# Moving the recurrence's decays, a weight's low parts and a pair's queries in the mixer of a decoder layer

## The chip, the cores and the metric

The kernel runs on one core of a Trainium2 chip. The metric is device time in microseconds (us) of one execution, the median over runs. Engines are named as in the profile: PE (TensorE, matrix products and transposes), PEld (its weight loads), DVE (VectorE), ACT (ScalarE), POOL (GpSimd), SP (SyncE, which issues DMA transfers).

## The reference

One layer of a decoder, on 512 tokens of 1024 channels, in float32: a SwiGLU feed-forward half step, a mixer, and a second half step, each between RMS norms. The change lies in the mixer, which joins a gated linear recurrence (RG-LRU, 512 channels) and sliding-window attention (8 query heads, 2 key and value heads of 64 channels, window 128, one sink per head):

```python
r = jax.nn.sigmoid(block_diag(xc, w_rg, b_rg))
i = jax.nn.sigmoid(block_diag(xc, w_ig, b_ig))
log_a = LRU_C * r * jax.nn.log_sigmoid(lam)
a = jnp.exp(log_a)
mult = jnp.sqrt(-jnp.expm1(2.0 * log_a))
u = mult * (i * xc)                     # h[t] = a[t] * h[t-1] + u[t]
...
scores = where(mask, q @ k_band * scale, MASK_VALUE)
m = jnp.maximum(jnp.max(scores), sink)
p = jnp.exp(scores - m)
out = (p / (jnp.sum(p) + jnp.exp(sink - m))) @ v_band
...
y_lru = h * jax.nn.gelu(gate_lru)
y = concatenate([rms_norm(y_lru, g_lru_out), rms_norm(out, g_attn_out)]) @ w_o
```

## The kernel before

Everything is kept transposed, channels on the 128 partitions and the 512 tokens along the free axis, so that one tile is 128x512. float32 products are made of three matmuls on rounded parts: a high part (a cast on ACT) and a low part (the value less its high part, on DVE) of the weight and of the input, as high by high, high by low, low by high (L407, L408, L409 in `mm3`).

**Weights.** They arrive by DMA into raw buffers, five of them, in a fixed order. `W.cast(n)` makes high parts on ACT (whi, L172) and `W.fill(n)` low parts on DVE (wlo, L177), up to n units beyond those taken by products. When the last unit of a raw buffer has been filled, the next load is issued on SP's queue.

**Order.** The schedule is manual: each engine runs its instructions in the order in which the program writes them, and semaphores alone hold one engine for another. So a statement's place in the program is its place in the queue of every engine that it uses.

**The recurrence** has four chunks of channels. `decay_a` (L1294) makes a = exp(ka r) on ACT and its square m on POOL (L1296); `decay_b` (L1299) makes (m + 1) th on DVE, `root` (L1302) its square root on ACT, `root_u` (L1305) multiplies it into the input on DVE, `scan` (L1308) runs the recurrence on DVE.

**Attention** runs in four pairs of heads, j = 0 to 3, with n = 0 and 1 for the two heads of a pair. `q_parts(j)` casts the queries out of PSUM (qTjh on ACT, L1313) and subtracts (qTjl on DVE, L1314). `products(j)` makes scores on PE (L1338). `scores` (L1344 to L1350) masks and takes maxima on DVE, `exps` (L1357, L1359) exponentiates on ACT, `normalise` (L1364 to L1366) scales on DVE. `turn_p` transposes on PE (L1374), copies to pa on ACT (L1376) and selects pc from it on POOL (L1377). `values(j)` multiplies by v (L1389 to L1396), `rows_high` and `rows_low` split the result into yah (ACT) and yal (DVE, L481), with squares (L438) summed in acc_attn (L1410).

**Fillers.** Between these steps PE runs the input products of later pairs and of gelu's gates, in the order pq2, gt0, pq3, gt1, gt2, gt3: `pump(n)` runs n steps of three matmuls each; eight steps make a product, and the eighth also issues `q_parts` (for a pq) or `gelu_a` (a copy and a square on ACT, L1419 and L1421, for a gt). `gelu_b` (L1424) and `gelu_d` are on DVE, `gelu_c` (tanh, L1427) on ACT.

**Tables.** ACT loads a table of functions when the next function isn't in the one loaded; `preload(f)` (L385) does so ahead of need, with an activation of one column. Exponential and tanh share a table, the square root has another.

After the last pair follow `values(3)`, the last gates, the norm of the recurrence's output, and the product with w_o (L1611), whose weights are also cast and split by W.

Of the kernel before, what the change touches and what calls it, by code (L numbers as in the profile page):

```python
# [11 lines left out]
AF = mybir.ActivationFunctionType  # L12
# [11 lines left out]
KC = C // P  # L24
# [97 lines left out]
def tile_layer(ctx: ExitStack, tc: tile.TileContext, out: bass.AP, **ins: bass.AP):  # L122
# [17 lines left out]
    def bank(name):  # L140
        return psum.tile([P, T], F32, tag="bank", name=name)

    def t2k(name, dt=F32):
        return big.tile([P, T], dt, tag="t2k", name=name, bufs=NT2K)

    def wt(name, w=T, dt=F32):
        return tmp.tile([P, w], dt, tag="w", name=name, bufs=NW)


    W = Weights()  # L150
# [233 lines left out]
    def preload(func):  # L384
        act.activation(dummy, eps, func)  # L385
# [25 lines left out]
    def product(w, xs, sl=ALL, name="", hooks=()):  # L411
        ps = bank(name)
        hooks = dict(hooks)
        for k, x in enumerate(xs):
            if k in hooks:
                hooks[k]()
            mm3(ps[:, sl], w, k, [t[:, sl] for t in x], k == 0, k == len(xs) - 1)
        return ps
# [829 lines left out]
    def in_product(name, hooks=(), ahead=AHEAD):  # L1248
        return product(W.take(ahead), mx.xs, name=name, hooks=hooks)
# [42 lines left out]
    def decay_a(ci):  # L1292
        a = rs_[ci]
        act.activation(a, a, AF.Exp, scale=ka[:, ci:ci + 1])  # L1294
        m = ms[ci] = wt(f"m{ci}")
        pool.tensor_mul(m, a, a)  # L1296

    def decay_b(ci):
        dve.scalar_tensor_tensor(th[ci], ms.pop(ci), 1.0, th[ci], op0=ALU.add, op1=ALU.mult)  # L1299

    def root(ci):
        act.activation(th[ci], th[ci], AF.Sqrt)  # L1302
# [16 lines left out]
    def q_parts(j, b):  # L1319
        qT[j] = in_parts(b, f"qT{j}")  # L1320
# [6 lines left out]
    def products(j):  # L1327

        for n in range(2):
            score_banks[j, n] = [bank(f"sc{j}{n}{i}") for i in range(2)]  # L1330
        (qh, ql), (kh, kl) = qT[j], kT
        rows = [slice(n * HD, (n + 1) * HD) for n in range(2)]
        for b in range(NB):
            i, o = ((1, 0), (0, 0), (0, 2 * P), (1, P))[b]
            blk, keys = slice(b * P, (b + 1) * P), slice(max(b - 1, 0) * P, (b + 1) * P)
            for p, (q_, k_) in enumerate(((qh, kh), (qh, kl), (ql, kh))):
                for n, pr in enumerate(rows):
                    pe.matmul(score_banks[j, n][i][:, o:o + keys.stop - keys.start], q_[pr, blk], k_[pr, keys], start=p == 0, stop=p == 2)  # L1338

    def scores(j, n):  # L1340
        h = n * KC + j
        mx_ = small.tile([P, NB], F32, tag="mx", name=f"mx{j}{n}")
        mid, ends = (t.rearrange("p (b k) -> p b k", k=P) for t in score_banks[j, n])
        dve.copy_predicated(mid[:, 1::2, :], up8[:, :2, :], mid[:, 0::2, :])  # L1344
        dve.tensor_reduce(mx_[:, 1:3], mid[:, 1::2, :], op=ALU.max, axis=AX.X)
        dve.copy_predicated(ends[:, 0, :], up8[:, 0, :], neg[:, :P])
        dve.copy_predicated(ends[:, 2, :], up8[:, 0, :], ends[:, 1, :])
        dve.tensor_reduce(mx_[:, 0::3], ends[:, 0::2, :], op=ALU.max, axis=AX.X)
        nm = small.tile([P, NB], F32, tag="nm", name=f"nm{j}{n}")
        dve.tensor_scalar(nm, mx_, -scale, nsink[:, h:h + 1], op0=ALU.mult, op1=ALU.min)  # L1350
        unit[j, n] = (ends[:, 0, :], mid[:, 1, :], mid[:, 3, :], ends[:, 2, :]), nm

    def exps(j, n):
        h, (blocks, nm) = n * KC + j, unit[j, n]
        den, es = (small.tile([P, NB], F32, tag=t, name=f"{t}{j}{n}") for t in ("den", "es"))
        sc = wt(f"sc{j}{n}")
        act.activation(es, nm, AF.Exp, bias=sinks[:, h:h + 1])  # L1357
        for b in range(NB):
            act.activation(sc[:, b * P:(b + 1) * P], blocks[b], AF.Exp, bias=nm[:, b:b + 1], scale=scale, accum_out=den[:, b:b + 1])  # L1359
        unit[j, n] = sc, den, es  # L1360

    def normalise(j, n):
        sc, den, es = unit[j, n]
        dve.tensor_add(den, den, es)  # L1364
        dve.reciprocal(den, den)
        dve.tensor_mul(v4(sc), v4(sc), den.unsqueeze(2).to_broadcast([P, NB, P]))  # L1366
        unit[j, n] = sc

    def turn_p(j, n):
        p = unit[j, n]  # L1370
        pt = bank(f"pt{j}{n}")
        for b in range(NB):
            bs = slice(b * P, (b + 1) * P)
            pe.transpose(pt[:, bs], p[:, bs], ident)  # L1374
        pa, pc = (t2k(f"{t}{j}{n}") for t in ("pa", "pc"))
        act.copy(pa, pt)  # L1376
        pool.affine_select(v4(pc)[:, 1:, :], v4(pa)[:, 1:, :], pattern=[[0, NB - 1], [1, P]], base=0, channel_multiplier=-1, compare_op=ALU.is_ge, fill=0.0)  # L1377
        unit[j, n] = pa, pc

    def values(j):  # L1380

        o = bank(f"po{j}")
        for b in range(NB):
            for n in range(2):
                pa, pc = unit[j, n]
                chans = slice(b * P + n * HD, b * P + (n + 1) * HD)
                keys, own = slice(b * P, min(b + 1 + (not b), NB) * P), slice(b * P, (b + 1) * P)
                if b:
                    pe.matmul(o[n * HD:(n + 1) * HD, own], vd[:, chans], pc[:, own], start=False, stop=b == NB - 1, skip_group_check=True)  # L1389
                else:  # L1390
                    pe.matmul(o[n * HD:(n + 1) * HD, keys], v[:, chans], pa[:, keys], start=True, stop=False, skip_group_check=True)
            for n in range(2):
                pa, pc = unit[j, n]
                chans, nxt = slice(b * P + n * HD, b * P + (n + 1) * HD), slice((b + 1) * P, (b + 2) * P)
                if 0 < b < NB - 1:
                    pe.matmul(o[n * HD:(n + 1) * HD, nxt], v[:, chans], pa[:, nxt], start=False, stop=False, skip_group_check=True)  # L1396
        po[j] = o

    def rows_high(j):
        ysp[KC + j] = t2k(f"yah{j}", F32R), t2k(f"yal{j}", F32R)  # L1400
        x_high(ysp[KC + j], po[j], col("g_attn_out", j), ALL)
        if j == 0:
            act.activation(acca, po[j], AF.Square)
        else:
            po["sq", j] = square(po[j], ALL, f"a{j}")

    def rows_low(j):
        x_low(ysp[KC + j], po[j], col("g_attn_out", j), ALL)
        if j:
            dve.tensor_add(acca, acca, po.pop(("sq", j)))  # L1410
# [44 lines left out]
    def pump(n):  # L1455
        for _ in range(n):
            next(steps, None)
# [24 lines left out]
    pv = in_product("pv", (), 0)  # L1482
    W.cast(2)
    preload(AF.Exp)
    for n in range(2):
        exps(0, n)
    vT = taken(wt("vT"), pv)
# [4 lines left out]
            pe.transpose(vt[:, b * P:(b + 1) * P], vT[:, b * P:(b + 1) * P], ident)  # L1492

    pq = in_product("pq1", {2: turn_v}, 0)
    normalise(0, 0)
    v, vd = t2k("v"), t2k("vd")
    dve.tensor_copy(v, vt)
    normalise(0, 1)
    W.fill(1)
    for ci in range(KC):  # L1500
        decay_a(ci)
    q_parts(1, pq)
    dve.tensor_sub(vd[:, P:], v[:, P:], v[:, :T - P])
    turn_p(0, 0)
    pump(1)
    turn_p(0, 1)
    products(1)
    W.cast(1)
    preload(AF.Sqrt)
    for ci in range(KC):  # L1510
        decay_b(ci)
        root(ci)
    W.fill(1)
    preload(AF.Exp)
    pump(4)

    after = {0: [(root_u, 0), (root_u, 1), (scan, 0)],
# [2 lines left out]
    for j in range(KC - 1):  # L1520
        for n in range(2):
            scores(j + 1, n)
            exps(j + 1, n)
        values(j)
        rows_high(j)
        W.fill(1)
        for n in range(2):
            normalise(j + 1, n)
        pump(4)
        W.cast(2)  # L1530
        rows_low(j)
        for fn, i in after[j]:
            fn(i)
        pump((5, 5, 6)[j])
        turn_p(j + 1, 0)
        pump(1)
        turn_p(j + 1, 1)
        if j < KC - 2:
            products(j + 2)
        W.fill(2)  # L1540
        pump(4)
# [191 lines left out]
```

## Time and profile before

| | |
|---|---|
| median of 3 runs | 861.47 us (861.0 to 862.05) |
| profiled execution | 859.76 us, of which span 857.7 us |
| granted TensorE clock, mean | 0.997 |
| busy shares of the span | PE 98%, PEld 90%, DVE 77%, ACT 62%, POOL 18% |
| instructions | 14130 |

The profile is one execution, seen by the hardware profiler; its span runs from the first instruction to the last, and the execution's own time is 2.06 us longer. In a row of a time line stand start (us from the span's start), duration, engine, line, operation, output<-inputs, shape and count; a count above 1 means that equal instructions in a row were put together, and the duration is then of all of them from the first start to the last end. In square brackets stands how long the engine had been idle before, and on what. In a row of the waits stand who waited, for whom, the total, the count and the mean. The mixer part that the change touches lies between about 395 and 460 us of the span.

### The profile page before, as it was taken

The numbers are of one execution on the slowest core, as the hardware profiler recorded it, in microseconds if no ns is written. First come the engines' busy times: TensorE is split into PE (matmuls) and PEld (weight loads), VectorE is DVE, ScalarE is ACT, GpSimd is POOL, SyncE is SP. The second block draws the span as 40 slices with busy tenths as digits, with TensorE's granted clock in tenths as the row PEclk, the third lists the DMA queues.
The fourth block names the chain that finished last, engine by engine and source line by source line (L and its number), as shares of the span: only waits on it lengthen the run. The fifth ranks groups of instructions, "written<-read, shape, count | busy, mean of one in ns | idle before, by whom it ended". The sixth has DMA issues, their size and how long they took to land.

```text
span 857.7 us, 14130 instructions
## 1 busy us (share of the span) xinstructions
PE 844.0 (98%) x5534; PEld 768.7 (90%) x5534; DVE 658.1 (77%) x897; ACT 529.1 (62%) x901; POOL 155.4 (18%) x185
## 2 busy tenths in 40 slices
PE   9999999999999999999989999999999999999996
PEld 8888999989989998998778889888998998998995
DVE  4989898887988866767888675357488789888856
ACT  6647567566566555658766776245466657657542
POOL 2022005014025021015203030001101303204412
PEclk9999999999999999999999999999999999999998
DMA  8265339739559463113060508244433946938912
GB/s 247 100 196 196 119 105 234 189 99 237 150 109 265 156 194 126 50 50 99 2 146 27 193 28 294 75 141 155 147 99 103 231 134 150 219 99 200 267 75 98
DMA packets 92901, 124.41 MB, mean 145 GB/s; under 512 B 5864, under 2 KB 62500, under 8 KB 92836
## 3 DMA queue, kind: packets, MB, share of 16 engines
q1 hardware_dynamic: 76276, 86.68, 32.5%
q0 software_dynamic: 16416, 36.71, 19.2%
q8 instruction: 43, 0.70, 0.3%
q14 instruction: 22, 0.18, 0.1%
q10 hardware_dynamic: 144, 0.13, 0.0%
HBM read 93.10 MB, written 30.41 MB: 144 GB/s over the span
## 4 chain that ended last, share of the span: by engine, by line
PE 90%; DVE 4%; ACT 3%; DMA 1%; SPq 1%; issue 0%; DVEq 0%; ACTq 0%
PE aa L817 12%; PE ab L817 11%; PE da L817 6%; PE db L817 5%; PE wo L1611 4%; PE ba L817 3%; PE bb L817 3%; PE mn L699 1%; PE an L699 1%; PE yal L1145 1%; PE yal L1146 1%; PE yb L1146 1%; PE yb L1144 1%; PE yal L1144 1%; PE yb L1145 1%; DMA raw_second<-in_ffn_w_gu 1%
## 5 line engine op out<-in xcount | busy, mean ns | idle before, releaser
L925 POOL DMA_DIRECT2D yp_b<-stage x42 | 36.4, 1133 | 149.8 <-ACT stage L922 141.1
L925 POOL DMA_DIRECT2D yp_a<-stage x42 | 37.0, 1163 | 146.1 <-ACT stage L922 141.3
L1173 POOL DMA_DIRECT2D yp_b<-stage x8 | 4.3, 541 | 91.8 <-ACT stage L1172 90.9
L1144 PE MATMUL yal<-whi_ad,hha 128*128 128x512 f32 x48 | 18.9, 393 | 0.0
L1146 PE MATMUL yal<-whi_ad,hla 128*128 128x512 f32 x48 | 18.7, 390 | 0.0
L1145 PE MATMUL yal<-wlo_ad,hha 128*128 128x512 f32 x48 | 18.7, 389 | 0.0
L1145 PE MATMUL yb<-wlo_bd,hhb 128*128 128x512 f32 x48 | 18.7, 389 | 0.0
L1146 PE MATMUL yb<-whi_bd,hlb 128*128 128x512 f32 x48 | 18.7, 389 | 0.0
L1144 PE MATMUL yb<-whi_bd,hhb 128*128 128x512 f32 x48 | 18.7, 389 | 0.0
L177 DVE TENSOR_TENSOR wlo_bd<-raw_bd,whi_bd 128x1024 fp32r<-128x1024 f32 x10 | 12.2, 1224 | 8.1 <-ACT whi_bd L172 8.1
L177 DVE TENSOR_TENSOR wlo_wo<-raw_wo,whi_wo 128x1024 fp32r<-128x1024 f32 x8 | 10.3, 1309 | 7.2 <-ACT whi_wo L172 7.2
L177 DVE TENSOR_TENSOR wlo_ad<-raw_ad,whi_ad 128x1024 fp32r<-128x1024 f32 x10 | 12.2, 1222 | 4.0 <-ACT whi_ad L172 4.0
L1289 POOL TENSOR_TENSOR xcl<-xc,xch 128x512 fp32r<-128x512 f32 x4 | 5.1, 1300 | 52.3 <-ACT xch L1288 52.3
L1377 POOL TENSOR_SCALAR_AFFINE_SELECT pc<-pa 128x384 f32<-128x384 f32 x8 | 6.6, 835 | 42.0 <-ACT pa L1376 41.9
L600 ACT ACTIVATE sqxr<-x_rows 128x512 f32<-128x512 f32 x16 | 10.0, 630 | 5.6 <-DVE x_rows L630 5.6
L409 PE MATMUL pq<-xh_mx,wlo_q 128*128 128x512 f32 x32 | 12.6, 394 | 0.9 <-DVE wlo_q L177 0.9
L407 PE MATMUL gt<-xh_mx,whi_gt 128*128 128x512 f32 x32 | 13.2, 412 | 0.0
L1145 PE MATMUL ybl<-wlo_bd,hhb 128*128 128x512 f32 (+1 forms) x36 | 13.2, 366 | 0.0
L1144 PE MATMUL ybl<-whi_bd,hhb 128*128 128x512 f32 (+1 forms) x36 | 13.2, 366 | 0.0
L1146 PE MATMUL ybl<-whi_bd,hlb 128*128 128x512 f32 (+1 forms) x36 | 13.2, 365 | 0.0
L407 PE MATMUL pq<-xh_mx,whi_q 128*128 128x512 f32 x32 | 13.0, 407 | 0.0
L550 POOL TENSOR_TENSOR xg_f<-xh_f,xl_f 128x256 f32<-128x256 f32 x8 | 5.8, 764 | 39.8 <-DVE xl_f L481 39.8
(1831 smaller groups left out, 3690.7 us busy)
## 6 DMA issues: line engine op xcount, KB each, us to landing
yp_a<-stage POOLq DMA_DIRECT2D x50, 256.0 KB, 7.2
yp_b<-stage POOLq DMA_DIRECT2D x50, 256.0 KB, 8.0
raw_ad<-in_ffn_w_down SPq DMA_DIRECT2D x4, 1024.0 KB
raw_bd<-in_ffn_w_down SPq DMA_DIRECT2D x4, 1024.0 KB
xn<-in_x SPq DMA_DIRECT2D x8, 256.0 KB, 2.9
x_rows<-in_x POOLq DMA_DIRECT2D x4, 512.0 KB, 12.2
yp_a<-yp_a POOLq DMA_DIRECT2D x8, 256.0 KB, 9.0
raw_q<-in_w_in SPq DMA_DIRECT2D x4, 512.0 KB, 4.1
```

The source lines that it names most:

```text
L177: low.tensor_sub(two(lo, x), x, two(hi.bitcast(F32), x))
L407: pe.matmul(ps, hi[:, k, :], xh, start=start, stop=False)
L409: pe.matmul(ps, lo[:, k, :], xh, start=False, stop=stop)
L600: act.activation(wt(f"sq{name}{self.name}{tb}{dh}"), src, AF.Square, accum_out=self.ss[name, tb][:, dh:dh + 1])
L699: pe.matmul(b[:, l], w[part][:, k, :], xs[k][xpart][:, l], start=k + part + xpart == 0, stop=stop and k == KD - 1)
L817: pe.matmul(o, w[:, k, js], x, start=first and i + j + k == 0, stop=k == 3 and i == 2, skip_group_check=True)
L925: pool.dma_start(o, st.rearrange("p (a b) -> p a b", a=2) if len(o.shape) == 3 else st, accum_op=ALU.add)
L1144: pe.matmul(ps, hh[:, blk], hi[:, k, cs], start=start, stop=False)
L1145: pe.matmul(ps, hh[:, blk], lo[:, k, cs], start=False, stop=False)
L1146: pe.matmul(ps, hl_[:, blk], hi[:, k, cs], start=False, stop=stop)
L1377: pool.affine_select(v4(pc)[:, 1:, :], v4(pa)[:, 1:, :], pattern=[[0, NB - 1], [1, P]], base=0, channel_multiplier=-1, compare_op=ALU.is_g ...
L1611: pe.matmul(wo_banks[tb][dh], x, w[:, k, :], start=start and k == 0 and w is hi and not xp, stop=stop and k == 1 and xp == 1, skip_group_c ...
```

## The change

Three groups of statements move; no operation is added or dropped, and the number of table loads stays three in this part.

1. Ahead of the first pair's exponentials, the four `decay_a` and the low part of the second pair's query weight (`W.fill(2)`). Both stood after the first pair's normalise.
2. Two `decay_b` ahead of `normalise(0, 0)` and two after `normalise(0, 1)`; then the table of the square root and two `root`, ahead of `q_parts(1)`; two more `root` between the two `turn_p`. All of these stood after `products(1)`. The exponential's table now comes back ahead of the gate's low part.
3. In the loop over pairs, `pump((4, 5, 4)[j])` and a `W.fill(1)` ahead of `W.cast(2)`, `rows_low` and the recurrence's steps in `after`, and `pump((5, 4, 6)[j])` behind them. With j = 0 the `W.fill(1)` makes the low part of the fourth pair's query weight; with j = 1 the fifth step of the pump is the eighth of pq3, which issues `q_parts(3)`. The order on PE stays the same.

```diff
--- before.py
+++ after.py
@@ -1482,6 +1482,9 @@
     pv = in_product("pv", (), 0)
     W.cast(2)
     preload(AF.Exp)
+    for ci in range(KC):
+        decay_a(ci)
+    W.fill(2)
     for n in range(2):
         exps(0, n)
     vT = taken(wt("vT"), pv)
@@ -1492,26 +1495,28 @@
             pe.transpose(vt[:, b * P:(b + 1) * P], vT[:, b * P:(b + 1) * P], ident)
 
     pq = in_product("pq1", {2: turn_v}, 0)
+    for ci in (0, 1):
+        decay_b(ci)
     normalise(0, 0)
     v, vd = t2k("v"), t2k("vd")
     dve.tensor_copy(v, vt)
     normalise(0, 1)
-    W.fill(1)
-    for ci in range(KC):
-        decay_a(ci)
+    for ci in (2, 3):
+        decay_b(ci)
+    preload(AF.Sqrt)
+    root(0)
+    root(1)
     q_parts(1, pq)
     dve.tensor_sub(vd[:, P:], v[:, P:], v[:, :T - P])
     turn_p(0, 0)
+    root(2)
+    root(3)
     pump(1)
     turn_p(0, 1)
     products(1)
     W.cast(1)
-    preload(AF.Sqrt)
-    for ci in range(KC):
-        decay_b(ci)
-        root(ci)
+    preload(AF.Exp)
     W.fill(1)
-    preload(AF.Exp)
     pump(4)
 
     after = {0: [(root_u, 0), (root_u, 1), (scan, 0)],
@@ -1526,12 +1531,13 @@
         W.fill(1)
         for n in range(2):
             normalise(j + 1, n)
-        pump(4)
+        pump((4, 5, 4)[j])
+        W.fill(1)
         W.cast(2)
         rows_low(j)
         for fn, i in after[j]:
             fn(i)
-        pump((5, 5, 6)[j])
+        pump((5, 4, 6)[j])
         turn_p(j + 1, 0)
         pump(1)
         turn_p(j + 1, 1)
```

The lines of the functions are the same in both kernels; behind the first hunk those of the changed kernel are some higher (v's copy L1502 for L1497).

On DVE, around the second pair's queries, before (den and sc belong to the two normalises, v and vd are the values, wlo_q the low part of the second pair's query weight):

```order
L1366 TENSOR_TENSOR sc_4553<-sc_4553,den_4551 128x512
L1497 COPY v<-vt 128x512
L1364 TENSOR_TENSOR den_4559<-den_4559,es_4560 128x4
L1365 RECIPROCAL den_4559<-den_4559 128x4
L1366 TENSOR_TENSOR sc_4561<-sc_4561,den_4559 128x512
L177 TENSOR_TENSOR wlo_q_4548<-raw_q_4412,whi_q_4547 128x1024
L1314 TENSOR_TENSOR qT1l<-pq_4570,qT1h 128x512
L1503 TENSOR_TENSOR vd<-v 128x384
L1299 SCALAR_TENSOR_TENSOR th_4431<-m_4610,th_4431 128x512
L1299 SCALAR_TENSOR_TENSOR th_4446<-m_4613,th_4446 128x512
L1299 SCALAR_TENSOR_TENSOR th_4489<-m_4616,th_4489 128x512
L1299 SCALAR_TENSOR_TENSOR th_4504<-m_4619,th_4504 128x512
```

And the same place of the changed kernel:

```order
L177 TENSOR_TENSOR wlo_q_4548<-raw_q_4412,whi_q_4547 128x1024
L1252 COPY vT<-pv 128x512
L1299 SCALAR_TENSOR_TENSOR th_4431<-m_4552,th_4431 128x512
L1299 SCALAR_TENSOR_TENSOR th_4446<-m_4555,th_4446 128x512
...
L1366 TENSOR_TENSOR sc_4566<-sc_4566,den_4564 128x512
L1502 COPY v<-vt 128x512
...
L1366 TENSOR_TENSOR sc_4574<-sc_4574,den_4572 128x512
L1299 SCALAR_TENSOR_TENSOR th_4489<-m_4558,th_4489 128x512
L1299 SCALAR_TENSOR_TENSOR th_4504<-m_4561,th_4504 128x512
L1314 TENSOR_TENSOR qT1l<-pq_4583,qT1h 128x512
```

The four decay_b now stand ahead of the queries' low part qT1l, two of them ahead of both normalises, and the weight's low part has gone from between to a place ahead of vT.

On ACT, from the decays (r) to the roots (th), with the second pair's queries and the copies pa between, before:

```order
L1294 ACTIVATE r_4426<-r_4426,ka 128x512
...
L1294 ACTIVATE r_4499<-r_4499,ka 128x512
L1313 CAST qT1h<-pq_4570 128x512
L1376 COPY pa_4631<-pt_4626 128x512
L1376 COPY pa_4644<-pt_4639 128x512
L172 CAST whi_gt_0_4676<-raw_gt__4416 128x1024
L385 ACT_TABLE_LOAD
L385 ACTIVATE dummy<-eps 128x1
L1302 ACTIVATE th_4431<-th_4431 128x512
L1302 ACTIVATE th_4446<-th_4446 128x512
```

And the changed kernel, where the decays have gone to a place ahead of the first pair's exponentials:

```order
L385 ACT_TABLE_LOAD
L385 ACTIVATE dummy<-eps 128x1
L1302 ACTIVATE th_4431<-th_4431 128x512
L1302 ACTIVATE th_4446<-th_4446 128x512
L1313 CAST qT1h<-pq_4583 128x512
L1376 COPY pa_4638<-pt_4633 128x512
L1302 ACTIVATE th_4489<-th_4489 128x512
L1302 ACTIVATE th_4504<-th_4504 128x512
L1376 COPY pa_4653<-pt_4648 128x512
L172 CAST whi_gt_0_4685<-raw_gt__4416 128x1024
L385 ACT_TABLE_LOAD
```

A table load and two roots have come ahead of qT1h, and the other two roots ahead of the second copy pa.

On DVE, around the fourth pair's queries, in the second pass of the loop, before (xc are the recurrence's inputs, of root_u and scan):

```order
L1366 TENSOR_TENSOR sc_4898<-sc_4898,den_4896 128x512
L481 SCALAR_TENSOR_TENSOR yal_4918<-po_4904,cols,yah_4917 128x512
L1410 TENSOR_TENSOR acc_attn<-acc_attn,sq_a_4920 128x512
L1305 TENSOR_TENSOR xc_4314<-xc_4314,th_4489 128x512
L1305 TENSOR_TENSOR xc_4316<-xc_4316,th_4504 128x512
L1308 SCALAR_TENSOR_TENSOR xc_4312<-r_4441,xc_4312 128x512
L1424 SCALAR_TENSOR_TENSOR gq_4860<-gq_4860,gt_4858 128x512
L1314 TENSOR_TENSOR qT3l<-pq_4862,qT3h 128x512
```

And the changed kernel:

```order
L1366 TENSOR_TENSOR sc_4898<-sc_4898,den_4896 128x512
L1314 TENSOR_TENSOR qT3l<-pq_4862,qT3h 128x512
L481 SCALAR_TENSOR_TENSOR yal_4918<-po_4904,cols,yah_4917 128x512
L1410 TENSOR_TENSOR acc_attn<-acc_attn,sq_a_4920 128x512
L1305 TENSOR_TENSOR xc_4314<-xc_4314,th_4489 128x512
L1305 TENSOR_TENSOR xc_4316<-xc_4316,th_4504 128x512
L1308 SCALAR_TENSOR_TENSOR xc_4312<-r_4441,xc_4312 128x512
L1424 SCALAR_TENSOR_TENSOR gq_4860<-gq_4860,gt_4858 128x512
```

The queries' low part has moved up past six operations, from gelu's step to a place right behind the third pair's second normalise.

## The prediction

> **What bounds the kernel now.** I read the page's busy line first, then the chain of work that ended last by engine, then the waits that end PE's idle time in the stage that the change touches, and then the time lines of PE, DVE, ACT and POOL between 398 and 486 us.
>
> ```profile
> PE 844.0 (98%) x5534; PEld 768.7 (90%) x5534; DVE 658.1 (77%) x897; ACT 529.1 (62%) x901; POOL 155.4 (18%) x185
> PE 90%; DVE 4%; ACT 3%; DMA 1%; SPq 1%; issue 0%; DVEq 0%; ACTq 0%
> PE sc L1338 <- ACT qT3h L1313: 2.0, 1, 2.0
> PE pq L409 <- DVE wlo_q L177: 0.9, 1, 0.9
> PE sc L1338 <- DVE qT3l L1314: 0.3, 1, 0.3
> ```
>
> PE is busy 98% of the span and carries 90% of the chain, so only PE's waits can be won. Three of them (total, count, mean in us) are of the kind that the change aims at: the fourth pair's score products wait 2.0 us for the query's high part and 0.3 us for its low part, and the fourth query product waits 0.9 us for its weight's low part. What such a wait is worth also depends on the next thing that PE would have to wait for.
>
> **The low part of the fourth query weight.**
>
> ```profile
> 427.27 0.51 PE L409 MATMUL pq<-xh_mx,wlo_q 128*128 128x512 f32 x1 [0.88 <-DVE wlo_q L177]
> 425.75 1.47 DVE L177 TENSOR_TENSOR wlo_q<-raw_q,whi_q 128x1024 fp32r<-128x1024 f32 x1
> 421.64 1.09 ACT L172 CAST whi_q<-raw_q 128x1024 fp32r<-128x1024 f32 x1
> ```
>
> PE waits 0.88 us. The subtraction stands on DVE behind yal0, two root_u and scan 0. Its cast ended at 421.64 + 1.09 = 422.73. Ahead of those four it can begin there and end, even at 1.47, at 424.2, 2.2 us before PE asks for it at 427.27 - 0.88 = 426.39. So the 0.88 goes. Those four start up to 1.5 us later; their readers (gelu, the LRU's output) come tens of us on, so I cost that at nothing on PE. If that cover were missing it would be the same 1.5 us on the chain of DVE, taken up below.
>
> **The fourth pair's queries.**
>
> ```profile
> 438.18 0.60 PE L1374 MATMUL pt<-ident,sc 128*128 128x128 f32 x4
> 440.81 0.33 PE L1338 MATMUL sc<-kTh,qT3h 64*128 64x128 f32 x2 [2.03 <-ACT qT3h L1313]
> 442.91 0.50 PE L407 MATMUL gt<-xh_mx,whi_gt 128*128 128x512 f32 x1
> 422.84 0.60 PE L1374 MATMUL pt<-ident,sc 128*128 128x128 f32 x4
> 424.96 0.50 PE L407 MATMUL gt<-xh_mx,whi_gt 128*128 128x512 f32 x1
> 434.09 0.39 PE L409 MATMUL pq<-xh_mx,wlo_q 128*128 128x512 f32 x1
> 434.63 0.61 ACT L438 ACTIVATE sq_a<-po 128x512 f32<-128x512 f32 x1
> 440.19 0.57 ACT L1313 CAST qT3h<-pq 128x512 fp32r<-128x512 f32 x1
> 440.79 0.69 DVE L1314 TENSOR_TENSOR qT3l<-pq,qT3h 128x512 fp32r<-128x512 f32 x1 [1.17 <-ACT qT3h L1313]
> ```
>
> From the last transposes ahead of the products to the first gate product behind them PE takes 442.91 - 438.18 = 4.73 us for the fourth pair, and 424.96 - 422.84 = 2.12 for the third, which waits for nothing: 2.61 are lost. The product's last matmul ended at 434.48, yet the cast stood on ACT behind gelu's tanh (gelu_c0), which follows yal1, two root_u, scan 1 and gelu_b0 on DVE. Now it stands behind the square that ends at 434.63 + 0.61 = 435.24, so qT3h is done at 435.8 and qT3l at 436.5, ahead of the 440.81 - 2.03 = 438.78 at which PE asks. The 2.61 go: 3.49 with the part above.
>
> **The decays.** This part moves work ahead of PE's products(1).
>
> ```profile
> 400.39 0.28 ACT L1357 ACTIVATE es<-nm,sinks 128x4 f32<-128x4 f32 x1
> 403.50 2.58 ACT L1294 ACTIVATE r<-r,ka 128x512 f32<-128x512 f32 x4
> 407.77 0.59 ACT L1313 CAST qT1h<-pq 128x512 fp32r<-128x512 f32 x1 [1.68 <-PE pq L409]
> 410.89 1.28 ACT L385 ACT_TABLE_LOAD   x1
> 412.29 2.18 ACT L1302 ACTIVATE th<-th 128x512 f32<-128x512 f32 x4
> 408.45 0.69 DVE L1314 TENSOR_TENSOR qT1l<-pq,qT1h 128x512 fp32r<-128x512 f32 x1 [0.55 <-ACT qT1h L1313]
> 409.45 0.27 PE L1338 MATMUL sc<-kTh,qT1l 64*128 64x128 f32 x2
> ```
>
> On ACT, qT1h now stands behind four decays (2.5 in pitch), two pairs' exponentials (403.50 - 400.39 = 3.11), a table load with its dummy (412.29 - 410.89 = 1.40) and two roots (half of 2.18, 1.05 in pitch): 400.39 + 2.5 + 3.11 + 1.40 + 1.05 = 408.45 instead of 407.77. The low part behind it had 409.45 - 409.14 = 0.31 to spare, so ACT alone makes PE wait 0.4 us.
>
> [...]
>
> On DVE two decay_b come ahead of pair 1's first normalise and two ahead of qT1l, with POOL's squares m beside them.
>
> ```profile
> 402.79 0.69 DVE L1366 TENSOR_TENSOR sc<-sc,den 128x512 f32<-128x512 f32 x1
> 403.65 0.69 DVE L1497 COPY v<-vt 128x512 f32<-128x512 f32 x1 [0.17 <-PE vt L1492]
> 404.65 1.27 DVE L1366 TENSOR_TENSOR sc<-sc,den 128x512 f32<-128x512 f32 x1
> 404.33 1.04 POOL L1296 TENSOR_TENSOR m<-r 128x512 f32<-128x512 f32 x1 [5.46 <-ACT r L1294]
> 404.33 5.47 POOL L1296 TENSOR_TENSOR m<-r 128x512 f32<-128x512 f32 x4 [5.46 <-ACT r L1294]
> 405.84 2.06 DVE L177 TENSOR_TENSOR wlo_q<-raw_q,whi_q 128x1024 fp32r<-128x1024 f32 x1
> 413.19 1.21 DVE L177 TENSOR_TENSOR wlo_gt<-raw_gt__4416,whi_gt 128x1024 fp32r<-128x1024 f32 x1
> 410.14 3.13 DVE L1299 SCALAR_TENSOR_TENSOR th<-m,th 128x512 f32<-128x512 f32 x4
> 438.95 0.67 DVE L1424 SCALAR_TENSOR_TENSOR gq<-gq,gt 128x512 f32<-128x512 f32 x1
> ```
>
> The same multiplication takes 0.69 while POOL is idle and 1.27 while the first m runs, ending 0.55 after it; a low part takes 2.06 beside m and 1.21 without; qT1l, which reads PSUM, takes its 0.69 beside m all the same. So a DVE operation with two SBUF inputs and an operation of POOL seem to take turns. The first decay ends at 400.39 + 0.65 = 401.04, its m at about 402.2 (an estimate: that end, 1.04, and the 0.1 to 0.2 between engines). From there DVE has four decay_b (0.67 each, as the same form takes in gelu_b0), two normalises (0.69 each), v with the second one's short operations (404.65 - 403.65 = 1.00) and some 0.35 for the short operations of the first: 2.7 + 1.4 + 0.35 + 1.0 = 5.4, to 407.6. The turns add the three later m, 3.1, less what of them runs beside v and the short operations, some 0.8: 409.9. Then qT1l takes 0.69, and PE reads it at 410.6: **a new wait of 1.1 us** in place of none. From below it is 0.4 (ACT alone). From above, with m at its mean beside DVE, 5.47/4 = 1.37, it is 3 x 0.33 = 1.0 more: 2.1. decay_b at 3.13/4 = 0.78 would add 0.4, which lies inside. I take 1.1, since the 1.04 is of an m that ran by turns. The low part wlo_q that stood between (2.06) now runs before vT, where DVE waited for PE: nothing.
>
> PE after products(3) thus stands at 1.1 - 3.49 = **-2.4 us**.
>
> **What is late next.**
>
> ```profile
> 414.33 0.42 DVE L1344 COPY_PREDICATED sc<-up,sc 128x256 f32<-128x256 uint8 x1
> 441.61 1.07 ACT L172 CAST whi_gt<-raw_gt__4849 128x1024 fp32r<-128x1024 f32 x1
> 444.29 0.41 DVE L1344 COPY_PREDICATED sc<-up,sc 128x256 f32<-128x256 uint8 x1
> 457.36 1.01 POOL L1377 TENSOR_SCALAR_AFFINE_SELECT pc<-pa 128x384 f32<-128x384 f32 x2 [14.07 <-ACT pa L1376]
> 459.43 0.39 PE L1389 MATMUL po<-pc,vd 128*64 128x128 f32 x4
> 484.47 2.36 DVE L177 TENSOR_TENSOR wlo_wo<-raw_wo,whi_wo 128x1024 fp32r<-128x1024 f32 x2 [4.58 <-ACT whi_wo L172]
> 485.99 0.39 PE L1611 MATMUL wo<-wlo_wo,ylh 128*128 128x512 f32 x1
> ```
>
> DVE and ACT form a second chain: scores, exponentials, normalise, copies, then gelu, the LRU's output and the weights of w_o. POOL's last select ends at 458.37 and PE reads it at 459.43, 1.06 later. The low part of a w_o weight ends at about 484.47 + 1.18 = 485.65 (half of 2.36; a start right behind puts it at 485.7) and PE reads it at 485.99: about 0.26 to spare. So PE keeps of its 2.4 only 0.26 plus whatever the second chain gains.
>
> That chain gains little. The scores of pair 2 (414.33) stood behind four decay_b and a low part; now they stand behind a low part that waits for its cast: the last decay_b ends at 409.9, root 3 (2.18/4 = 0.55) and pa01 (0.6, as the casts of its shape) at about 411.1, the cast takes 1.05 and the subtraction 1.21, so 413.35, **1.0 earlier**. In the loop it gives most of this back. gelu_b0 ended at 438.95 + 0.67 = 439.62 and now has qT3l ahead of it: 440.24. ACT behind it does without the cast of qT3h (0.57), so the cast whi_gt ends at 442.75 instead of 441.61 + 1.07 = 442.68. One low part of 1.21 follows it, with 0.1 between engines; the other one that came right behind qT3l is done by then: scores(3) at 444.05, **0.2 earlier**. At the end of the mixer the gain lies between the 0.2 here and the 1.0 at pair 2's scores, since work of both stages feeds it; nearer to the later place, I take 0.45, so the end moves by -0.45 - 0.26 = **-0.7 us**.
>
> The profiled execution took 859.76 us (its span is 857.7), so it becomes 859.1; the median of the runs lies 1.71 above that execution, at 861.47, and becomes **860.8**.
>
> **The rivals.**
>
> A. *The gates do not hold.* PE's 2.4 us reach the end: 861.47 - 2.4 = 859.1. For it speaks that PE waits for nothing at 459.43 and 485.99 now and carries 90% of the chain; against it the 1.06 and 0.26 us above, less than 2.4. It needs a second chain that moves as PE does.
>
> B. *Slower: the wait that the change adds at products(1) also delays the second chain.* If DVE's turns come at their upper end (2.1), the last two decay_b end about 1 us later, roots 2 and 3 behind them too, and on ACT these now stand ahead of pa01 and the cast whi_gt: pa01 ends at about 412.8, the cast at 413.8, the low part at 415.0, so scores(1) start at 415.0 instead of 414.33. That is 1.7 later than in my forecast; carried through to scores(3) it makes -0.2 into +1.45, and with the 0.26 the end moves by +1.2: 862.6. It decides when scores(1) start after about 413.85 (forecast 413.35 plus the 0.5 that the chain may lose). For it speaks that both engines lie close there; against it that a single m took 1.04. It would come true likewise if the first root started later behind the load than the row's 1.40, and of B's chance I give that 0.02. [...]
>
> C. *Milder.* DVE and POOL do not take turns in this order, only ACT delays the queries (0.4), and the second chain keeps about 0.5 us more: -1.2, 860.3. For it: qT1l beside m took 0.69; against it the two slow rows.
>
> D. *One of the two waits stays*, say because yal0 still comes ahead of the low part. Then PE has 1.5 to 2.6 us less to give, but the second chain sets the end as before, so the time stays near the forecast or, with both left, 1.1 above before, 862.6. The written order leaves no room for the latter, and I count it within B.
>
> **How the numbers follow.** Forecast 0.58, A 0.14, B 0.14, C 0.14. About 0.2% (1.72 us) is what a measurement of this kernel can tell from no change: faster means below 859.75, slower above 863.19. Faster: nearly all of A, a fifth of C and a little of the forecast, 0.13 + 0.03 + 0.03 = 0.19. Slower: a third of B, and 0.02 for the forecast's upper tail, 0.07. The rest, 0.74, is within. The range goes from 858.9, which takes in half of A, to 862.7, which takes in B's value: outside are half of A and of B's part above, and the forecast's tails, about 0.2.
>
> **What the next profile should show.** At the fourth pq's low matmuls and at sc with qT3h and qT3l no wait is left on PE (pt to gt around products(3) back at 2.1). At sc with qT1l there is a new wait near 1.1 for DVE, and beside m decay_b and normalise are near 1.2 each. scores(1) begin near 413.4 and scores(3) near 444.1. PE waits at po for pc near 1 us, and again at the w_o products: the gain is given back there. The forecast is wrong if those two gates show no wait while the end has moved by more than 1.7 us, or if scores(1) begin later than 413.85.

## The result and the profile after

The changed kernel takes 858.5 us (median of 8 runs, 858.15 to 859.21), the kernel before 860.91 in the runs beside it (8 runs, 859.18 to 862.33). The ratio is 0.9974, 95% interval 0.9963 to 0.9985: 2.4 us faster, where the prediction had 0.7 and a range whose lower end, 858.9, lies 0.4 above what came. The profiled execution took 858.53 us (span 856.3), only 1.23 less than the profiled execution before (859.76). That the medians differ by twice as much as the two profiles is the riddle of this case.

The busy line of the page, after,

```profile
PE 845.0 (99%) x5534; PEld 768.4 (90%) x5534; DVE 656.8 (77%) x897; ACT 529.2 (62%) x901; POOL 153.6 (18%) x185
```

and the waits of PE between 395 and 500 us:

```profile
PE sc L1338 <- DVE qT1l L1314: 0.7, 1, 0.7
PE po L1391 <- ACT pa L1376: 0.4, 1, 0.4
```

The three waits of before are gone, and two smaller ones have come, at products(1) and at values(3). PE's time line after, at the places of the prediction (this execution is 0.25 us ahead from its first 25 us on, so that much is to be taken off each comparison; the product with w_o is L1617 here and L1611 before):

```profile
410.29 0.33 PE L1338 MATMUL sc<-kTh,qT1l 64*128 64x128 f32 x2 [0.72 <-DVE qT1l L1314]
427.14 0.39 PE L409 MATMUL pq<-xh_mx,wlo_q 128*128 128x512 f32 x1
437.94 0.60 PE L1374 MATMUL pt<-ident,sc 128*128 128x128 f32 x4
438.46 0.33 PE L1338 MATMUL sc<-kTh,qT3h 64*128 64x128 f32 x2
440.07 0.50 PE L407 MATMUL gt<-xh_mx,whi_gt 128*128 128x512 f32 x1
456.58 0.92 PE L1391 MATMUL po<-pa,v 128*64 128x256 f32 x3 [0.41 <-ACT pa L1376]
458.89 0.50 PE L1617 MATMUL wo<-whi_wo,yah 128*128 128x512 f32 x1
484.77 0.50 PE L1617 MATMUL wo<-wlo_wo,ylh 128*128 128x512 f32 x1
485.11 0.39 PE L1617 MATMUL wo<-whi_wo,ylh 128*128 128x512 f32 x1
```

and before, at the two of these places that the prediction does not show:

```profile
460.62 0.50 PE L1611 MATMUL wo<-whi_wo,yah 128*128 128x512 f32 x1
486.22 0.39 PE L1611 MATMUL wo<-whi_wo,ylh 128*128 128x512 f32 x1
```

From pt to gt around products(3) stand 440.07 - 437.94 = 2.13 us in place of 4.73. At gt PE is 442.91 - 440.07 = 2.84 ahead of before, 2.59 without the head start. At the first product with w_o, right behind values(3), it is 460.62 - 458.89 = 1.73 ahead. At the later one with a low part it is 485.99 - 484.77 = 1.22 ahead, 0.97 without the head start, and one row on 486.22 - 485.11 = 1.11, or 0.86, where it stays to the end: 1.7 us were given back, 1.1 of them at values(3) and the rest at w_o's low parts.

The second chain after, first DVE's time line,

```profile
402.20 2.77 DVE L1299 SCALAR_TENSOR_TENSOR th<-m,th 128x512 f32<-128x512 f32 x2
404.89 0.99 DVE L1364 TENSOR_TENSOR den<-den,es 128x4 f32<-128x4 f32 x1
407.34 0.15 DVE L1364 TENSOR_TENSOR den<-den,es 128x4 f32<-128x4 f32 x1
408.35 1.28 DVE L1299 SCALAR_TENSOR_TENSOR th<-m,th 128x512 f32<-128x512 f32 x2
409.56 0.68 DVE L1314 TENSOR_TENSOR qT1l<-pq,qT1h 128x512 fp32r<-128x512 f32 x1
413.00 0.42 DVE L1344 COPY_PREDICATED sc<-up,sc 128x256 f32<-128x256 uint8 x1
434.89 0.69 DVE L1314 TENSOR_TENSOR qT3l<-pq,qT3h 128x512 fp32r<-128x512 f32 x1 [0.56 <-ACT qT3h L1313]
443.51 0.42 DVE L1344 COPY_PREDICATED sc<-up,sc 128x256 f32<-128x256 uint8 x1
```

and POOL's time line:

```profile
400.93 4.93 POOL L1296 TENSOR_TENSOR m<-r 128x512 f32<-128x512 f32 x4 [2.32 <-ACT r L1294]
```

Two decay_b take 2.77 us beside the squares m and 1.28 once POOL is done. The short operation den takes 0.99 beside the last m and ends at 405.88, with POOL (400.93 + 4.93 = 405.86); the next den takes 0.15. Both fit the turns of the two engines that the prediction read from the rows of before. Scores of pair 2 start at 413.00 and those of pair 4 at 443.51, 1.1 and 0.5 earlier than before without the head start.

### The profile page after: what moved, and what is told of

Same layout as the page of the kernel before. It is cut to its first block, busy times and chain, and to the rows that moved or that the text cites. A ratio compares the mean times of both kernels' runs of the same rounds, so it can differ in the third digit from the quotient of the medians.

```text
span 856.3 us, 14126 instructions
## 1 busy us (share of the span) xinstructions
PE 845.0 (99%) x5534; PEld 768.4 (90%) x5534; DVE 656.8 (77%) x897; ACT 529.2 (62%) x901; POOL 153.6 (18%) x185
## 5 line engine op out<-in xcount | busy, mean ns | idle before, releaser
L1691 ACT ACTIVATE ysq<-yp_b 128x512 f32<-128x512 f32 (+1 forms) x9 | 5.2, 582 | 12.4 <-DVE yp_b L1690 11.7
```

## The experiments

Medians below have the runs of the kernel before beside them: 860.94 us in the first four experiments (35 runs), 861.27 in the next four (15), 861.18 in the last three (21). Each kernel ran on the same chip as the runs of the kernel before that stand beside it.

**1. The kernel before, again.** No edit.

> The kernel before, unchanged. It asks where the 1.15 us lie that the median of its eight runs (860.91) has over its profiled execution (859.76), while the changed kernel's median is its profiled time. Theory N (noise of the measurement): the ratio is 1.000 with an interval of about 0.001, the spread of both is some 3 us, and another profiled execution shows the same waits in the mixer as the first, with what it is longer by at its start or end or spread over the span. Theory V (the kernel before has a stage of its own that varies): a longer execution shows it as a larger wait of PE at one place in the mixer, say qT3h at 3 us and more instead of 2.0.

Measured: 861.52 us (12 runs), ratio 1.0 (0.999 to 1.0009). The profiled execution, of 861.7 us, waits for the same things as the first one, qT3h again by 2.0. It differs from it behind that wait. First the time line of this execution, then of the first one:

```profile
441.27 0.33 PE L1338 MATMUL sc<-kTh,qT3h 64*128 64x128 f32 x2 [2.01 <-ACT qT3h L1313]
443.66 0.79 PE L407 MATMUL gt<-xh_mx,whi_gt 128*128 128x512 f32 x1
444.25 0.63 PE L408 MATMUL gt<-xl_mx,whi_gt 128*128 128x512 f32 x1
444.68 0.63 PE L409 MATMUL gt<-xh_mx,wlo_gt 128*128 128x512 f32 x1
...
446.38 0.40 PE L407 MATMUL gt<-xh_mx,whi_gt 128*128 128x512 f32 x1
446.62 0.40 PE L408 MATMUL gt<-xl_mx,whi_gt 128*128 128x512 f32 x1
```

```profile
443.25 0.40 PE L408 MATMUL gt<-xl_mx,whi_gt 128*128 128x512 f32 x1
443.49 0.39 PE L409 MATMUL gt<-xh_mx,wlo_gt 128*128 128x512 f32 x1
```

The same matmuls start 444.68 - 444.25 = 0.43 us apart instead of 0.24, until 446.38, and then at 0.24 again. The granted clock is 0.83 from 441 to 444 us and 0.60 from 444 to 447, where the first execution has 1.00 in both; with 446.38 - 444 = 2.38 us of the last stretch at the slow pitch, it is there 1 - 0.40 x 3 / 2.38 = 0.50, half the clock, and in the mixer it comes only there. The table of windows has the whole stretch (stretch, its length, PE's busy time, instructions, granted clock, DMA share, GB/s), first for this execution, then for the profiled one before:

```profile
10.00:20.00 10.00, 10.00 (x75) 0.86 0.99 298
435.00:447.00 12.00, 9.71 (x56) 0.86 0.46 83
```

```profile
10.00:20.00 10.00, 10.00 (x86) 1.00 0.99 299
435.00:447.00 12.00, 9.69 (x75) 1.00 0.43 89
```

The granted clock falls to 0.86 of full speed over the 12 us around products(3), which is some 3.4 us at half (0.14 x 12 / 0.5), and in the kernel's first 20 us; elsewhere up to the last matmul it is 1.00. PE is 0.46 us behind the first profile ahead of the drop (441.27 against 440.81) and 1.9 at the end (spans of 859.6 and 857.7), so the drop behind the wait cost 1.4 us. Neither Theory N nor Theory V as I had put them: the wait is the same, and what varies is the clock that follows it.

A mean clock of 0.997 or more marks an execution without such a drop, called undisturbed below: 3.4 us at half speed take 0.002 off the mean. The profiles of this study bear it out: from 0 to 20 and from 435 to 462 us the eight at 0.997 or more have no drop, and the five below have one or two. Of 71 runs of the kernel before beside the experiments 18 have it, with a median of 859.45, near the profiled 859.76; the other 53 have a median of 861.36. Of the changed kernel's 8 runs 6 have it, median 858.45. So the change is worth 1.0 us where no drop is involved, and the rest of the 2.4 would be that its median execution has no drop while that of before has one. The fifth experiment tests this.

**2. The loop's moves alone.**

```diff
-        pump(4)
+        pump((4, 5, 4)[j])
+        W.fill(1)
         W.cast(2)
...
-        pump((5, 5, 6)[j])
+        pump((5, 4, 6)[j])
```

> Only the moves in the loop (low part of the fourth query weight and the fourth pair's queries early); the decays as before. Theory G (the chain of DVE and ACT sets the end): PE stands 3.5 us or a little more earlier behind products(3), and then waits about 2 us for pa at values(3) and again at the w_o weights; mixer end and time -0.2 to -0.5 us. Theory P (PE's own waits set the end): -3.5 us, no wait behind products(3).

Measured: 859.47 us (11 runs), ratio 0.9987 (0.9979 to 0.9996); undisturbed (8 of 11) 859.29, 0.15 below before's 859.45. This kernel's wait at values(3):

```profile
PE po L1391 <- ACT pa L1376: 1.8, 1, 1.8
```

PE's 3.5 us are lost again at the gates, as Theory G says. It had 0.2 to 0.5 us for the time; the undisturbed runs give 0.15, and the median falls by 1.5, by this reading through the clock.

**3. The decays alone.** The changed kernel with the loop as before.

> Only the decays, roots and the second pair's low part moved; the loop as before. Theory G: the wait of about 0.7 to 1.1 us at products(1) is there, the DVE chain runs 1 us earlier behind it, qT3h comes 1 us earlier so that this wait shrinks to about 1.3, and the end moves by -0.8 to -1.0 us, as in the whole change, although both waits of the loop stay. Theory P: slower by the new wait, +0.7 to +1.1 us, or no change at best.

Measured: 858.82 us (12 runs), ratio 0.9979 (0.997 to 0.9989); undisturbed (4 of 12) 858.04, 1.4 below before. Theory P has the wrong sign. The part that gives PE a new wait is the one that wins undisturbed time, which fits Theory G, where it moves the second chain; the size is above the 0.8 to 1.0 expected. It is also 0.4 more than the whole change wins (858.45; six runs against four here): on top of the decays the loop's moves seem to cost undisturbed time, and they win in the median through the clock. Its remaining wait, for which 1.3 us was expected:

```profile
PE sc L1338 <- ACT qT3h L1313: 0.9, 1, 0.9
```

and its window around products(3):

```profile
435.00:447.00 12.00, 10.77 (x62) 0.86 0.42 98
```

The clock drops behind this 0.9 us wait too in its profiled execution. Of the 12 runs 8 are below 0.997, but only three of them, the profiled one among these, lie 2.2 us or more above the undisturbed; the other five lie 0.6 to 1.1 above, about what a drop at the start alone goes with in the sixth experiment.

**4. The second pair's queries ahead of the roots.**

```diff
+    q_parts(1, pq)
     for ci in (2, 3):
         decay_b(ci)
     preload(AF.Sqrt)
     root(0)
     root(1)
-    q_parts(1, pq)
```

> The whole change, but the second pair's queries are cast ahead of the last two decay_b, the table of the square root and the two roots, so that the new wait at products(1) goes. Theory G: PE is 1 us earlier behind products(1), but the decays and roots come later than in the change, the chain of DVE and ACT behind them too: time between that of the change and +1.5 us above it. Theory P: 0.7 to 1.1 us faster than the change, about 3.5 below the kernel before.

Measured: 859.78 us (11 runs), ratio 0.9993 (0.9985 to 1.0002); undisturbed (7 of 11) 859.66, 1.2 slower than the change, though it takes the new wait at products(1) away. This is Theory G. Its profiled execution waits 1.8 us at values(3), and there the clock falls instead:

```profile
456.00:462.00 6.00, 4.34 (x26) 0.73 0.00 0
```

**5. The wait filled.** The kernel before, and in `products`:

```diff
+        if j == 3:
+            for _ in range(8):
+                pe.matmul(score_banks[3, 0][0], kT[0][:, :P], mx.xs[0][0], start=True, stop=True)
```

> The kernel before with eight extra matmuls of 128x512 (8 x 0.23 = 1.8 us) ahead of products(3), where PE waits 2.0 us for qT3h; their result is overwritten. Nothing else moves. Theory C (while PE waits there, the granted clock is cut to half in most executions, and the 128x512 matmuls behind the wait come every 0.43 instead of 0.23 us for 1.4 us or more): with the wait filled the clock stays, executions with a mean clock below 0.997 become rare, and the median falls from 860.9 to about 859.5, though PE has more work and arrives no earlier. Theory N (the clock changes at random places, not for this wait): the median stays at 860.9, with about three of four executions below 0.997.

Measured: 859.56 us (11 runs) against 861.27, ratio 0.9982 (0.9973 to 0.9991), 10 of 11 runs at 0.997 or more, against 4 of 15 of the kernel before beside it. The fill (2.10 us for the eight) and the matmuls behind it:

```profile
438.42 2.10 PE L1333 MATMUL sc<-xh_mx,kTh 128*128 128x512 f32 x8
440.70 0.33 PE L1341 MATMUL sc<-kTh,qT3h 64*128 64x128 f32 x2 [0.18 <-ACT qT3h L1313]
...
443.14 0.40 PE L408 MATMUL gt<-xl_mx,whi_gt 128*128 128x512 f32 x1
443.38 0.39 PE L409 MATMUL gt<-xh_mx,wlo_gt 128*128 128x512 f32 x1
```

The score products start only 0.1 us earlier than in the first profile, as does the rest of this stage, nothing else moved, and 1.7 us are gone from the median: Theory C is shown. With PE's idle time at this place filled, the granted clock stays at 1.00 from 435 to 447 us.

**6. The decays alone, filled.** Experiment 3 with the same lines and four matmuls.

> The decays part alone (as in the third experiment) with four extra matmuls (0.9 us) ahead of products(3), where 0.9 us of wait was left. Theory C: the executions below 0.997, 8 of 12 without the fill, become rare, and the median falls from 858.8 to the 858.0 of the undisturbed ones. Theory N: 858.8 as before.

Measured: 858.19 us (5 runs), ratio 0.9968 (0.9955 to 0.998); 3 of 5 at 0.997 or more, median 858.03. The other two, at 859.0, are 1 us above; the profiled one, at 0.995, has its drop in the first 20 us alone (0.94 from 0 to 10, 0.89 from 10 to 20, 1.00 from 435 to 462 us). So there are two places where the clock can be low. No run here is at 0.994, where experiment 3 had three of 12, and the profile has no drop at products(3); five runs are too few to show that the fill closes that place. Runs below 0.997 did not become rare, as Theory C had it, since the start brings some of its own.

**7. The change, PE delayed.** In `in_steps`:

```diff
         w = W.take(0)
         b = bank(name)
+        if name == "gt2":
+            for _ in range(2):
+                mm3(b, w, 0, mx.xs[0], True, True)
```

> The whole change with six extra matmuls (6 x 0.23 = 1.36 us) at the start of gt2, behind products(3); their result is overwritten. Theory G (the chain of DVE and ACT sets the end, PE gives back 1.7 us at values(3) and at the w_o weights): the time stays, at 858.5 +- 0.3, and the waits for pa and for the low parts of w_o vanish. Theory P (PE sets the end): 859.9.

Measured: 858.59 us (5 runs). 1.36 us more work for PE cost 0.1, and the only wait left in the mixer is that at products(1). This is Theory G: PE's lead is worth nothing in the change.

**8. The copies pa first.** The change, and:

```diff
-             2: [(scan, 2), (gelu_d, 0), (gelu_b, 1), (gelu_c, 1)]}
+             2: [(scan, 2), (gelu_d, 0)]}
...
+    gelu_b(1)
+    gelu_c(1)
     W.cast(3)
```

> The whole change, and gelu_b1 and gelu_c1 moved from ahead of the last pair's transposes and copies pa to behind them, so that the copies pa on ACT no longer stand behind gelu_b1 on DVE and gelu's tanh. Theory G: the gate at values(3) opens 1.2 us or more earlier, PE keeps its lead, and the time falls by up to 1.7 us, to about 856.8. Theory P: no change, 858.5.

Measured: 857.38 us (5 runs), ratio 0.9954 (0.9941 to 0.9966); 2 of 5 undisturbed at 856.64, 1.8 below the change's 858.45. The gate in its profile, on PE's time line:

```profile
456.03 0.65 PE L1391 MATMUL po<-pa,v 128*64 128x256 f32 x4
```

and ACT's time line ahead of it:

```profile
453.37 0.59 ACT L1376 COPY pa<-pt 128x512 f32<-128x512 f32 x1 [0.38 <-PE pt L1374]
```

The copies are done by 453.96, and values(3) no longer waits. PE keeps its lead to the end (span 854.6, 1.7 less than the change). This is Theory G, with the 1.7 that PE had given back. The median fell by 1.1 only: the other three runs, at 857.38 to 857.87, are below 0.997, and no profile shows where their clock drops.

**9. The low part alone.** The kernel before, and for j = 0 a `W.fill(1)` ahead of `W.cast(2)`.

> The kernel before with only the low part of the fourth query weight made early; queries and decays as before. PE's wait of 0.9 us for it goes. Theory G: the chain of DVE and ACT is 0.2 us later for it, the wait for qT3h grows from 2.0 to about 3.6 us, and undisturbed executions take 0.2 us more than before (859.6). Theory C on top: with a longer wait at least as many executions fall below a mean clock of 0.997 as before (about three of four), so the median is at or above before's 861. Theory P: 0.9 us faster.

Measured: 861.57 us (11 runs), ratio 1.0008 (0.9999 to 1.0017); no run of 11 reaches 0.997. From its profile, the wait:

```profile
PE sc L1338 <- ACT qT3h L1313: 3.3, 1, 3.3
```

and the window around it:

```profile
435.00:447.00 12.00, 8.46 (x51) 0.86 0.14 39
```

The 0.9 us that PE no longer waits for the weight it waits for the query, and 0.4 more, and now no run keeps its clock. The undisturbed 0.2 of Theory G can't be read, since there was no such run; the other half of the expectation came.

**10. The queries alone.** Experiment 2 without the `W.fill(1)`.

> The kernel before with only the fourth pair's queries made early; low part and decays as before. Theory G: PE's wait for wlo_q of 0.9 us stays, those for qT3h and qT3l go, PE waits about 2 us at values(3) instead, and undisturbed executions take 0.4 us less than before (859.0). Theory C on top: fewer executions below 0.997 than before, median 859.0 to 859.5, so 1.5 to 2 us below before. Theory P: 2.6 us faster also in undisturbed executions.

Measured: 859.14 us (11 runs), ratio 0.9978 (0.9969 to 0.9987); 10 of 11 undisturbed, median 859.13: 0.3 below before's 859.45, and 2.0 below before's median. This is Theory G and Theory C together. PE waits 1.0 at values(3), less than the 2 expected.

**11. The copies pa first, without the early low part.** Experiment 8 without the `W.fill(1)`.

> The version with the copies pa first (eighth experiment), without the early low part of the fourth query weight. Theory G: DVE has 1 us of lead at that place from the decays, so PE waits for nothing there; undisturbed executions the same as in the eighth experiment (856.6) within 0.2, median 856.7 to 857.4. Theory P: 0.9 us slower than the eighth, since PE's wait for the low part comes back.

Measured: 856.98 us (5 runs), ratio 0.9951 (0.9939 to 0.9964), 4.2 below before; 3 of 5 undisturbed, 856.57. PE doesn't wait for the low part here. The undisturbed runs differ by 0.07 from those of experiment 8, within their spread; these two are the fastest versions of this study.

## Why the prediction was wrong

**The waits that go: right.** Both went in full, 0.88 and 2.6 us.

**The new wait: right.** I had 1.1 us for PE at products(1) from the turns of DVE and POOL. The start of sc with qT1l is 410.29 - 409.45 = 0.84 us later than before, though PE was 0.07 ahead at the transposes just above (408.58 against 408.65): 0.91 lost, of which 0.72 shows as the wait. Those transposes had lost 0.18 of the head start already (they wait for the second normalise, which two decay_b now precede), so the 1.1 came in full.

**The gates: right.** I had PE's 2.4 us come down to 0.26 and what the second chain gains. PE was 2.6 ahead and ended 0.86 ahead; experiment 7 shows that its lead was free to spend, and experiment 8 that the gate at values(3) held it. The chain gained 0.5 at pair 4's scores where I had 0.2, which goes with the 0.86 in place of 0.7. That rival A's figure, 859.1, lies nearer to what was measured is chance: in A PE's lead reaches the end, and it does not. Of the other rivals, B did not come (scores(1) begin at 413.00, ahead of 413.85, and the first root starts 407.26 - 405.86 = 1.40 behind its load, as before), C neither (the turns are there), nor D (both waits went). Two slips of the prediction change nothing. By the forecast's own steps B's pa01 ends at 409.9 + 1.0 + 0.55 + 0.6 = 412.1 and not at 412.8, so its price should have been some 0.7 less. And the exponentials that cost 3.11 on ACT are those of the two heads of one pair, not of two pairs. Neither of the forecast's signs of being wrong came: they asked the profile alone, which went much as expected, and not how far the median lies from it.

**The step that failed** is the last of the sum: "the median of the runs lies 1.71 above that execution, at 861.47, and becomes 860.8". I took the distance between median and profiled execution for a constant that the change leaves alone. It was in the main the price of one of the waits that the change removes. Behind a stall of PE at products(3) the clock is halved for about 3.4 us in most executions (11 of 15 are below a mean of 0.997 beside experiment 5, and 1 of 11 with the wait filled), which costs 1.4, and the one that was profiled is of the few without it. The removed wait was worth its 2.0 us to PE, most of which the gates took back, and 1.4 us of clock in the median. The kernel before pays those to its end, since its PE waits for nothing between products(3) and the end of the mixer: in experiment 1 it is 1.9 us behind at the end as it is right behind the drop. Terms: 1.0 undisturbed (forecast 0.7) plus 1.4 of clock (forecast none) are the 2.4. The hint stood in what I had: three runs that all lay 1.2 to 2.3 above the profiled execution.

The trace shows the half (matmuls 0.43 us apart against 0.24, and the 0.50 worked out from the granted clock) and the length (from about 443.0 to 446.4), both in experiment 1. What sets them, and why the same wait has a drop behind it in some executions only, no run here shows. A wait of 2.0 us sufficed in most runs, and one of 0.9 in the profiled execution of experiment 3 (0.86 from 435 to 447 us). Nor does the length of the wait alone seem to decide: with 1.8 us at values(3), in experiments 2 and 4, 8 of 11 and 7 of 11 runs are undisturbed, against 18 of 71 with 2.0 at products(3). Around the wait at products(3) PE also runs transposes and score products of 64x128 and 64x256; whether those have a part in it no run here separates.

## What to carry to other kernels

Before a forecast is put against a median, ask what the profiled execution lacks: when the runs lie above it by more than they lie apart, look for a stall of the busiest engine behind which the granted clock falls, and price the stall as wait plus drop (here 2.0 and 1.4 us). A stall that cannot be removed can be filled with matmuls whose result is overwritten, which here won 1.7 us at no other cost. And time won on the busiest engine ahead of a gate is worth only what the chain behind the gate gains (here 0.86 of 2.6 us reached the end); moving the gate (experiment 8) then gives the rest.

## What was not expected of the hardware

- The clock halves for about 3.4 us behind a wait of 2.0 us of PE, in most executions of the same kernel (53 of 71 below a mean of 0.997, some of them by the kernel's start), and all 11 runs of the kernel with a wait of 3.3 us are below it. With a wait of 1.8 us at another place it is 3 and 4 runs of 11.
- The first 20 us have a low clock in some executions as well (0.86 from 10 to 20 us against 1.00), which goes with up to about 1 us (859.0 against 858.03 in experiment 6), with no drop in the mixer. Why it comes in some executions no run here shows.
- Two decay_b took 2.77 us while POOL's multiplications ran and 1.28 without, and an operation of 128x4 took 0.99 instead of 0.15, ending with POOL's: as if DVE and POOL took turns.
